# One transformer block: the seven-product stage of the second MLP matrix, reordered, with turned signs and two of its four sums formed by adding transfers

## The chip, the cores and the metric

The kernel runs on one core of one Trainium2 chip. The time is the device time of one execution in microseconds. The kernel before took 2019.21 us, the median of 3 runs (2017.92 to 2019.24).

## What is computed

One trunk layer on 512 tokens of width 2048, all in float32:

```
h = layer_norm(x, ln_in_g, ln_in_b)
u = h @ w_in                                   # pool values | q | k | v
m = concat(multi_scale_pool(u_pool), stick_breaking_attention(q, k, v)) @ w_out
h = layer_norm(2**0.25 * h + m, ln1_g, ln1_b)
f = square(relu(h @ w_ff1 + b_ff1))            # 512 x 8192
f = f @ w_ff2 + b_ff2                          # the stage that is changed
h = layer_norm(2**0.25 * h + f, ln2_g, ln2_b)
```

Only the product `f @ w_ff2` (8192 x 2048, "W_2" below) and the sums that go into it are changed.

## The kernel before

A float32 product is made of three matmuls of rounded parts: each operand is split into a high part (a copy to the type fp32r, on ScalarE) and a low part (the rest, a subtraction on VectorE), and `three` (L280 to L284) issues high x high, high x low and low x high into one bank of PSUM.

W_2's stage saves products in the manner of Strassen and Winograd: f and W_2 are cut into 2 x 2 blocks, and 7 block products take the place of 8. The inner dimension of 8192 is cut into 16 blocks of 512, four blocks make a slice (`slice_of`, L764), and there are four slices s = 0 to 3. A block is a unit u = 0 to 3 of its slice. W_2's 2048 columns are four groups q of 512: groups 0 and 1 are the left half, 2 and 3 the right half. One pass n = 0 or 1 takes the column pair (n, n + 2). For each (n, u) there are four pieces of W_2, 512 KB each: b11 and b12 (upper half of the inner block, left and right column), b21 and b22 (lower half).

The products, with A for blocks of f: P1 = A11 b11; P5 = S1 (b12 - b11); P6 = S2 (b22 - b12 + b11); P3 = S4 b22; P7 = S3 (the sum of P6, less b11); P2 = A12 b21; P4 = A22 (b21 less the sum of P6). S1 to S4 are sums of blocks of f. One product of one (n, u) is 12 matmuls, so a slice has 7 x 2 x 4 x 12 = 672, and the stage 2688.

How the pieces travel:

- `operands` (L678) runs after each block of the stage before. It squares the ReLU, forms S1 to S4 on VectorE (L690), splits all seven and writes them to DRAM (`f_d`, GpSimd's queue, L698).
- `operand` (L721) loads them again, 512 KB per unit and operand, through GpSimd's queue into a ring of 16 buffers named `o` (L716); four of these are free during the stage before.
- `w2_unit` (L731) loads a piece of W_2 through SyncE's queue into a ring of 10 buffers (tag `raw`, 3 + 7). b11 is loaded twice, once for P1 and once for P7 (tile `b11b`).
- `parts` (L739) splits a piece: `th` on ScalarE (L743), `tl` on VectorE (L744). The split tiles have 2 + 2 buffers each.
- The running sum of a unit sits in a tile `c` of its own (tag `c{n}{u}`). VectorE changes it or reads it four times per (n, u), 128 x 1024 elements each: L788 in `five`, L797 in `six_three`, L807 in `seven`, L825 in `four`.
- The banks of PSUM are two pairs `x` and two pairs `v` or `w`, all eight. `accumulate` (L756) adds a finished product to the output tiles `acc`.

The order of the work is set by the code's order and by a scheduler that places what stands under `high_priority` (L767) earlier than written; each engine and each queue then runs its own list in order. A slice runs P1 and P5 for n = 0, then n = 1; P6 and P3; P7; P2 and P4, each with n as the outer loop. The last slice runs P2, the first two normed output blocks (`norm_out`, L902), P7 and P4 at its end, and P4 is done by halves of the tokens.

Of the kernel before, what the change touches and what calls it, by code (L numbers as in the profile page):

```python
# [9 lines left out]
F32 = mybir.dt.float32  # L10
F32R = mybir.dt.float32r
AF = mybir.ActivationFunctionType
ALU = mybir.AluOpType
# [10 lines left out]
def block_kernel(  # L24
# [60 lines left out]
    def f(ap):  # L85
        return ap.bitcast(F32)
# [578 lines left out]


    mixing.close()
    first = pool(ctx, "first", 4, side="right")
# [9 lines left out]
    def operands(b, banks):  # L678
# [41 lines left out]

    def operand(s, *os):  # L721

        ops = [[] for _ in os]
        for u in range(PER):
            for n, o in enumerate(os):
                t = place(f"o{s}_{o}_{u}")
                nc.gpsimd.dma_start(f(t), f_d[s][u][o].rearrange("h p t -> p h t"))  # L727
                ops[n].append(t.rearrange("p h (i t) -> p h i t", i=2))
        return ops

    def w2_unit(b, half, q, name):  # L731

        k0 = b * N + half * H2
        early_one = turn("raw", 3, 10)
        raw = (wp if early_one else right).tile([P, 2, N], F32, tag="raw", bufs=3 if early_one else 7, name=name)
        nc.sync.dma_start(raw, w2[k0:k0 + H2, q * N:(q + 1) * N].rearrange("(c p) n -> p c n", p=P))
        return raw

    def parts(t, name, ring=False):  # L739
# [24 lines left out]
    def slice_of(s):  # L764
# [4 lines left out]
        x = [pair(f"x{s}_{n}", f"x{n}") for n in range(2)]  # L769
        v = [pair(f"v{s}_{n}", f"v{n}") for n in range(2)]  # L770
        chain = {}
# [11 lines left out]
        def five(n, u, b11):  # L783
            b, at, e = step(n, u)
            with ahead():
                b12 = w2_unit(b, 0, n + 2, f"b12_{at}")
                c = chain[n, u] = right.tile([P, 2, N], F32, tag=f"c{n}{u}", bufs=1, name=f"c_{at}")
                nc.vector.tensor_tensor(c, b12, b11, op=ALU.subtract)  # L788
                p5 = parts(c, f"5_{at}")
# [21 lines left out]
        def two(n, u):  # L811
            b, at, e = step(n, u)
            with ahead():
                b21 = w2_unit(b, 1, n, f"b21_{at}")
                p2 = parts(b21, f"2_{at}")
            times(w[n], A12, u, p2, *e)
            return b21

        def four(n, u, b21=None, ring=False):
            b, at, _ = step(n, u)  # L820
            with ahead():
                if b21 is None:
                    b21 = w2_unit(b, 1, n, f"b21b_{at}")
                c = chain[n, u]
                nc.vector.tensor_tensor(c, b21, c, op=ALU.subtract)  # L825
                return parts(c, f"4_{at}", ring)

        with ahead():
            A11, S1 = operand(s, 0, 3)
        for n in range(2):  # L830
            if s == 0 and n == 0:
                for us in (0, 1), (2, 3):
                    for u, b11 in [(u, one(n, u)) for u in us]:
                        five(n, u, b11)
            else:
                for u in units:
                    five(n, u, one(n, u))
            accumulate(x[n], 0, n)
            accumulate(v[n], 2, n + 2)
        with ahead():  # L840
            S2, S4 = operand(s, 4, 6)
        for n in range(2):
            for u in units:
                six_three(n, u)
            accumulate(x[n], 0, n + 2)
            accumulate(v[n], 0, n + 2)
        w = [pair(f"w{s}_{n}", f"v{n}") for n in range(2)]
        if not end:
            with ahead():
                S3, = operand(s, 5)  # L850
            for n in range(2):
                for u in units:
                    seven(n, u)
                accumulate(x[n], 2, n + 2)
            with ahead():
                A12, A22 = operand(s, 1, 2)
            for n in range(2):
                for u in units:
                    b21 = two(n, u)
                    times(x[n], A22, u, four(n, u, b21), False, u == PER - 1)  # L860
                accumulate(w[n], 0, n)
                accumulate(x[n], 2, n)
            return
        with ahead():
            A12, = operand(s, 1)
        for n in range(2):
            for u in units:
                two(n, u)
            accumulate(w[n], 0, n)
# [5 lines left out]
        for n in range(2):  # L875
            for u in units:
                seven(n, u)
            accumulate(x[n], 2, n + 2)
        with ahead():
            A22, = operand(s, 2)  # L880
        p4 = {}
        for t in range(2):
            for n in range(2):
                for u in units:
                    if t == 0:
                        p4[n, u] = four(n, u, ring=n == 1)
# [61 lines left out]
```

## Time and profile before

| | us |
|---|---|
| median of 3 runs | 2019.21 |
| the profiled execution, whole | 2015.19 |
| its span, first to last instruction | 2013.5 |
| W_2's stage, from the first of its matmuls | 1329.3 |
| its last matmul ends | 1997.0 |
| matmuls of the stage | 2688 |

The span is what the rows are measured in. The profiled execution is 4 us below the median of the runs, so a difference found in the rows is taken from 2019.21 and not from the span. TensorE is busy for nearly the whole span, and its matmuls overlap, so what counts in it is how many matmuls a stretch holds and where it sat idle. In slice 0 of the stage the share of the 16 DMA engines' time that packets took is near or above 1.00 (packets of two queues overlap on an engine).

### The profile page before, as it was taken

The numbers are of one execution on the slowest core, as the hardware profiler recorded it, in microseconds if no ns is written. First come the engines' busy times: TensorE is split into PE (matmuls) and PEld (weight loads), VectorE is DVE, ScalarE is ACT, GpSimd is POOL, SyncE is SP. The second block draws the span as 40 slices with busy tenths as digits, with TensorE's granted clock in tenths as the row PEclk, the third lists the DMA queues.
The fourth block names the chain that finished last, engine by engine and source line by source line (L and its number), as shares of the span: only waits on it lengthen the run. The fifth ranks groups of instructions, "written<-read, shape, count | busy, mean of one in ns | idle before, by whom it ended". The sixth has DMA issues, their size and how long they took to land.

```text
span 2013.5 us, 22312 instructions
## 1 busy us (share of the span) xinstructions
PE 1937.6 (96%) x8736; PEld 1592.4 (79%) x8736; DVE 1214.1 (60%) x1513; ACT 737.7 (37%) x898; POOL 169.3 (8%) x222
## 2 busy tenths in 40 slices
PE   6999999999999999999999999978999999999995
PEld 4888888877889988888888888856888778778874
DVE  8445565675459644544444444446977677678689
ACT  3344555552124233333333333323333333333331
POOL 5000000000000110010000001021111101101100
PEclk8999999999999999999999999989999999999998
DMA  5122222235344455556555556659676567577562
GB/s 221 32 86 82 84 84 84 74 99 188 105 141 135 159 188 169 174 182 207 191 175 168 167 170 210 201 202 370 216 263 226 176 233 242 178 238 242 194 224 84
DMA packets 157225, 345.47 MB, mean 172 GB/s; under 512 B 10688, under 2 KB 28224, under 8 KB 156736
## 3 DMA queue, kind: packets, MB, share of 16 engines
q1 hardware_dynamic: 124912, 224.43, 34.5%
q0 software_dynamic: 32064, 119.55, 16.4%
q8 instruction: 69, 1.13, 0.2%
q14 instruction: 36, 0.29, 0.0%
q10 hardware_dynamic: 144, 0.07, 0.0%
HBM read 281.09 MB, written 62.91 MB: 171 GB/s over the span
## 4 chain that ended last, share of the span: by engine, by line
PE 46%; issue 25%; DVE 14%; DMA 12%; POOL 2%; SPq 1%; ACT 0%; DVEq 0%; POOLq 0%; ACTq 0%
PE qk L361 9%; DMA b<-in_w_ff_dram 8%; PE f L210 7%; PE o L210 6%; DVE tl L744 5%; PE p L210 4%; DMA b11b<-in_w_ff_dram 4%; PE x L283 4%; PE o L283 3%; PE v L283 3%; PE f L283 2%; PE v L210 2%; POOL f_d L698 2%; DVE b11b L807 1%; DVE acc L759 1%
## 5 line engine op out<-in xcount | busy, mean ns | idle before, releaser
L210 PE MATMUL f<-h1l,wh_f 128*128 128x512 f32 x960 | 373.5, 389 | 0.0
L210 PE MATMUL f<-h1h,wh_f 128*128 128x512 f32 x960 | 373.5, 389 | 0.0
L210 PE MATMUL f<-h1h,wl_f 128*128 128x512 f32 x960 | 349.1, 389 | 0.0
L184 DVE TENSOR_TENSOR wl_f<-raw_f,wh_f 128x1024 fp32r<-128x1024 f32 x120 | 146.8, 1224 | 325.0 <-ACT wh_f L183 325.0
L283 PE MATMUL x<-th,o 128*128 128x512 f32 x1024 | 332.9, 394 | 9.1 <-DMA o<-f_d 7.2
L183 ACT CAST wh_f<-raw_f 128x1024 fp32r<-128x1024 f32 x120 | 126.4, 1053 | 392.1 <-PE f L210 374.2
L283 PEld LDWEIGHTS x<-th,o 128*128 128x128 f32 x1024 | 193.3, 189 | 52.5 <-issue 7.6
L283 PE MATMUL x<-tl,o 128*128 128x512 f32 x512 | 203.3, 397 | 11.9 <-DVE tl L744 11.9
L210 PEld LDWEIGHTS f<-h1h,wh_f 128*128 128x128 f32 x960 | 180.3, 188 | 37.5
L210 PEld LDWEIGHTS f<-h1h,wl_f 128*128 128x128 f32 x960 | 180.1, 188 | 37.4
L210 PEld LDWEIGHTS f<-h1l,wh_f 128*128 128x128 f32 x960 | 180.2, 188 | 37.3
L283 PE MATMUL v<-th,o 128*128 128x512 f32 x512 | 169.7, 395 | 7.4 <-ACT th L743 7.4
L743 ACT CAST th<-b 128x1024 fp32r<-128x1024 f32 x96 | 101.1, 1053 | 188.8 <-PE v L283 59.2
L743 ACT CAST th<-c 128x1024 fp32r<-128x1024 f32 x96 | 100.8, 1052 | 161.9 <-PE x L283 109.8
L744 DVE TENSOR_TENSOR tl<-b,th 128x1024 fp32r<-128x1024 f32 x96 | 116.9, 1219 | 25.4 <-ACT th L743 25.4
L698 POOL DMA_DIRECT2D f_d<-fh x32 | 30.4, 951 | 1209.6 <-ACT fh L695 1209.6
L283 PEld LDWEIGHTS x<-tl,o 128*128 128x128 f32 x512 | 96.9, 189 | 39.7 <-DVE tl L744 18.8
L744 DVE TENSOR_TENSOR tl<-c,th 128x1024 fp32r<-128x1024 f32 x96 | 116.8, 1219 | 14.0 <-ACT th L743 13.8
L727 POOL DMA_DIRECT2D o<-f_d x112 | 81.2, 725 | 491.6 <-PE x L283 299.8
L283 PEld LDWEIGHTS v<-th,o 128*128 128x128 f32 x512 | 97.1, 190 | 29.0 <-ACT th L743 8.2
L283 PE MATMUL v<-tl,o 128*128 128x512 f32 x256 | 101.8, 398 | 7.8 <-DVE tl L744 7.7
L361 PE MATMUL qk<-hTl,wh_qk 128*128 128x512 f32 x256 | 99.9, 390 | 0.0
(208 smaller groups left out, 3243.4 us busy)
## 6 DMA issues: line engine op xcount, KB each, us to landing
b<-in_w_ff_dram SPq DMA_DIRECT2D x128, 512.0 KB, 4.8
raw_f<-in_w_ff_dram SPq DMA_DIRECT2D x120, 512.0 KB, 3.9
o<-f_d POOLq DMA_DIRECT2D x112, 512.0 KB, 5.6
f_d<-fh POOLq DMA_DIRECT2D x32, 896.0 KB, 5.7
f_d<-fl POOLq DMA_DIRECT2D x32, 896.0 KB, 9.4
raw_qk<-in_w_in_dram SPq DMA_DIRECT2D x64, 256.0 KB, 2.9
b11b<-in_w_ff_dram SPq DMA_DIRECT2D x32, 512.0 KB, 4.2
raw_o<-in_w_out_dram SPq DMA_DIRECT2D x24, 512.0 KB, 3.7
```

The costliest lines, as they stand in the source:

```text
L183: nc.scalar.copy(h, raw)
L184: nc.vector.tensor_tensor(l, raw, f(h), op=ALU.subtract)
L210: mm = nc.tensor.matmul(bank, a, b, start=first and n == 0, stop=last and n == 2)
L283: mm = nc.tensor.matmul(bank, l, r, start=first and n == 0, stop=last and n == 2, skip_group_check=free)
L361: nc.tensor.matmul(bank, a, b, start=kc == 0 and n == 0, stop=kc == KC - 1 and n == 2)
L698: nc.gpsimd.dma_start(f_d[b // PER][b % PER][:, n, :, i * H2:(i + 1) * H2].rearrange("o p t -> p o t"), f(t))
L727: nc.gpsimd.dma_start(f(t), f_d[s][u][o].rearrange("h p t -> p h t"))
L743: nc.scalar.copy(h, t)
L744: nc.vector.tensor_tensor(l, t, f(h), op=ALU.subtract)
L759: nc.vector.tensor_tensor(a, a, banks[t], op=ALU.add)
L807: nc.vector.tensor_tensor(b11, chain[n, u], b11, op=ALU.subtract)
```

## The change

The pieces' sums are now all positive: S1, S2 and S4 are formed with the other sign, and the right half of the output is subtracted instead of added. So P5 takes b11 + b12, P6 that plus b22, P7 b22 + b12, and P4 the sum of P6 plus b21. A sum of two pieces can then be made by a transfer that adds to what lies in its destination, and two of the four are: b12 is added to b11's tile for P5 (but for the first three pieces of slice 0), and b12 is added to b22's tile for P7. These adding transfers are issued on GpSimd's queue. In the last slice P4's sum is formed so too. b11 is loaded straight into its `c` tile, and its second load is gone.

In each product the column pairs n = 0, 1 now are the inner loop and the units the outer one. In slices 0 to 2 P4 of a unit comes ahead of its P2. The last slice begins with P2. In slice 0 the loads of S2 and S4 wait for the second P1.

```diff
-        for o, x, y, op in ((s1, a21, a22, ALU.add), (s2, s1, a11, ALU.subtract),
-                            (s3, a11, a21, ALU.subtract), (s4, a12, s2, ALU.subtract)):
-            nc.vector.tensor_tensor(o, x, y, op=op)
+        nc.vector.tensor_tensor(s1, a22, a21, op=ALU.subtract)
+        nc.vector.scalar_tensor_tensor(s2, s1, -1.0, a11, op0=ALU.mult, op1=ALU.subtract)
+        nc.vector.tensor_tensor(s3, a11, a21, op=ALU.subtract)
+        nc.vector.scalar_tensor_tensor(s4, s2, -1.0, a12, op0=ALU.mult, op1=ALU.subtract)
...
+    def add_unit(t, b, half, q):
+        nc.gpsimd.dma_start(t, w2_at(b, half, q), accum_op=ALU.add)
...
-            nc.vector.tensor_tensor(a, a, banks[t], op=ALU.add)
+            nc.vector.tensor_tensor(a, a, banks[t], op=ALU.add if q < 2 else ALU.subtract)
...
         def one(n, u):
             b, at, e = step(n, u)
             with ahead():
-                b11 = w2_unit(b, 0, n, f"b11_{at}")
-                p1 = parts(b11, f"1_{at}")
-            times(x[n], A11, u, p1, *e)
-            return b11
+                if s == 0 and 2 * u + n < 3:
+                    b11[n, u] = w2_unit(b, 0, n, f"b11_{at}")
+                    p1 = parts(b11[n, u], f"1_{at}")
+                else:
+                    c = chain[n, u] = right.tile([P, 2, N], F32, tag=f"c{n}{u}", bufs=1, name=f"c_{at}")
+                    nc.sync.dma_start(c, w2_at(b, 0, n))
+                    p1 = parts(c, f"1_{at}")
+                    add_unit(c, b, 0, n + 2)
+            begun.append(times(x[n], A11, u, p1, *e))
...
-        def six_three(n, u):
+        def six(n, u):
...
-                b22 = w2_unit(b, 1, n + 2, f"b22_{at}")
+                b22[n, u] = w2_unit(b, 1, n + 2, f"b22_{at}")
                 c = chain[n, u]
-                nc.vector.tensor_tensor(c, b22, c, op=ALU.subtract)
+                nc.vector.tensor_tensor(c, c, b22[n, u], op=ALU.add)
                 p6 = parts(c, f"6_{at}")
-                p3 = parts(b22, f"3_{at}")
+                if end:
+                    add_unit(c, b, 1, n)
             times(x[n], S2, u, p6, False, u == PER - 1)
+
+        def three_(n, u):
+            with ahead():
+                p3 = parts(b22[n, u], f"3_{s}_{n}_{u}")
+                add_unit(b22[n, u], s * PER + u, 0, n + 2)
             times(v[n], S4, u, p3, False, u == PER - 1)
 
         def seven(n, u):
...
-                b11 = w2_unit(b, 0, n, f"b11b_{at}")
-                nc.vector.tensor_tensor(b11, chain[n, u], b11, op=ALU.subtract)
-                p7 = parts(b11, f"7_{at}")
+                p7 = parts(b22[n, u], f"7_{at}")
...
+        if end:
+            w = [pair(f"w{s}_{n}", f"v{n}") for n in range(2)]
+            with ahead():
+                A12, = operand(s, 1)
+            both(two, units)
+            every(w, 0, 0)
...
-        for n in range(2):
-            if s == 0 and n == 0:
-                for us in (0, 1), (2, 3):
-                    for u, b11 in [(u, one(n, u)) for u in us]:
-                        five(n, u, b11)
-            else:
-                for u in units:
-                    five(n, u, one(n, u))
+        for us in (0, 1), (2, 3):
+            both(one, us)
+            both(five, us)
...
-            S2, S4 = operand(s, 4, 6)
-        for n in range(2):
-            for u in units:
-                six_three(n, u)
+            S2, S4 = operand(s, 4, 6, behind=None if s else begun[1])
+        for u in units:
+            both(six, (u,))
+            both(three_, (u,))
...
-            for n in range(2):
-                for u in units:
-                    seven(n, u)
-                accumulate(x[n], 2, n + 2)
+            both(seven, units)
+            every(x, 2, 2)
             with ahead():
-                A12, A22 = operand(s, 1, 2)
-            for n in range(2):
-                for u in units:
-                    b21 = two(n, u)
-                    times(x[n], A22, u, four(n, u, b21), False, u == PER - 1)
+                A22, A12 = operand(s, 2, 1)
+            for u in units:
+                both(two, (u,), both(four, (u,)))
```

Two places where the lists of the engines change. Names are tile, slice, and for W_2's tiles pass n and unit u; `o0_4_1` is operand 4 (S2) of unit 1 in slice 0.

VectorE, slice 1, around P7. Before:

```order
L744 TENSOR_TENSOR tl_6_1_1_0_11280<-c_1_1_0_10980,th_6_1_1_0_11279 128x1024
L807 TENSOR_TENSOR b11b_1_1_1_11529<-c_1_1_1_11018,b11b_1_1_1_11529 128x1024
L744 TENSOR_TENSOR tl_3_1_1_0_11284<-b22_1_1_0_11276,th_3_1_1_0_11283 128x1024
L759 TENSOR_TENSOR acc0_3674<-acc0_3674,x1_0_0_10780 128x512
L759 TENSOR_TENSOR acc1_3675<-acc1_3675,x1_0_1_10781 128x512
L744 TENSOR_TENSOR tl_6_1_1_1_11315<-c_1_1_1_11018,th_6_1_1_1_11314 128x1024
L759 TENSOR_TENSOR acc0_3674<-acc0_3674,v1_0_0_10784 128x512
L759 TENSOR_TENSOR acc1_3675<-acc1_3675,v1_0_1_10785 128x512
L807 TENSOR_TENSOR b11b_1_1_2_11548<-c_1_1_2_11056,b11b_1_1_2_11548 128x1024
```

And after the change, VectorE, slice 1, P7:

```order
L756 TENSOR_TENSOR tl_7_1_0_0_11386<-b22_1_0_0_11077,th_7_1_0_0_11385 128x1024
L771 TENSOR_TENSOR acc0_3674<-acc0_3674,x1_1_0_10751 128x512
L771 TENSOR_TENSOR acc1_3675<-acc1_3675,x1_1_1_10752 128x512
L756 TENSOR_TENSOR tl_7_1_1_0_11402<-b22_1_1_0_11096,th_7_1_1_0_11401 128x1024
L771 TENSOR_TENSOR acc0_3674<-acc0_3674,v1_0_0_10753 128x512
L848 TENSOR_TENSOR c_1_0_1_10811<-c_1_0_1_10811,b21_1_0_1_11603 128x1024
L771 TENSOR_TENSOR acc1_3675<-acc1_3675,v1_0_1_10754 128x512
L756 TENSOR_TENSOR tl_7_1_0_1_11418<-b22_1_0_1_11149,th_7_1_0_1_11417 128x1024
```

Before, the subtraction of `b11b` for P7 stood among the splits of P6 and P3, eight places ahead of its own split; now P7's splits read `b22` as it is, and the additions of `b21` for P4 stand among them.

GpSimd's queue at the start of slice 0. Before:

```order
L727 DMA o0_6_2_10014<-f_d0_2_5519 128x2x512
L727 DMA o0_4_3_10016<-f_d0_3_5520 128x2x512
L727 DMA o0_6_3_10018<-f_d0_3_5520 128x2x512
L727 DMA o0_5_0_10312<-f_d0_0_5517 128x2x512
L727 DMA o0_5_1_10314<-f_d0_1_5518 128x2x512
L727 DMA o0_5_2_10316<-f_d0_2_5519 128x2x512
```

And after:

```order
L731 DMA o0_6_2_9999<-f_d0_2_5519 128x2x512
L731 DMA o0_4_3_10001<-f_d0_3_5520 128x2x512
L731 DMA o0_6_3_10003<-f_d0_3_5520 128x2x512
L749 DMA c_0_1_1_9746<-in_w_ff2_dram 128x2x512
L731 DMA o0_5_1_10307<-f_d0_1_5518 128x2x512
L749 DMA c_0_0_2_9841<-in_w_ff2_dram 128x2x512
L731 DMA o0_5_2_10309<-f_d0_2_5519 128x2x512
L749 DMA c_0_1_2_9860<-in_w_ff2_dram 128x2x512
L731 DMA o0_2_0_10445<-f_d0_0_5517 128x2x512
L749 DMA c_0_0_3_9879<-in_w_ff2_dram 128x2x512
L731 DMA o0_5_3_10311<-f_d0_3_5520 128x2x512
L749 DMA c_0_1_3_9898<-in_w_ff2_dram 128x2x512
```

The five adding transfers that P5 of slice 0 needs (L749) stand behind all twelve operand loads of P1, P5, P6 and P3; before, P5's second pieces came through SyncE's queue.

## Rows read from the trace of the kernel before

**Rows 1.** The profile's page, busy time by engine.
```profile
PE 1937.6 (96%) x8736; PEld 1592.4 (79%) x8736; DVE 1214.1 (60%) x1513; ACT 737.7 (37%) x898; POOL 169.3 (8%) x222
```

**Rows 2.** Stretches: length, busy us (count) by engine, granted clock, DMA share, GB/s.
```profile
core 0: us, PE busy (x) PEld busy (x) DVE busy (x) ACT busy (x) POOL busy (x), PEclk, DMA share, GB/s
1329.30:1511.30 182.00, 161.74 (x672) 129.31 (x673) 134.71 (x130) 63.98 (x61) 32.03 (x43) 0.94 0.79 283
1511.30:1673.60 162.30, 156.36 (x673) 125.31 (x673) 118.89 (x116) 58.98 (x56) 20.27 (x28) 1.00 0.66 222
1673.60:1836.00 162.40, 157.05 (x673) 125.16 (x672) 118.81 (x116) 58.96 (x56) 20.28 (x28) 1.00 0.66 219
1836.00:1997.00 161.00, 155.11 (x673) 125.44 (x672) 130.11 (x154) 56.09 (x56) 11.60 (x17) 1.00 0.53 176
1450.00:1500.00 50.00, 50.00 (x219) 40.69 (x218) 37.45 (x38) 18.97 (x18) 5.07 (x7) 1.00 0.73 247
1340.00:1350.00 10.00, 4.85 (x12) 3.09 (x12) 3.62 (x4) 1.43 (x2) 6.03 (x8) 0.67 1.00 339
1340.00:1400.00 60.00, 46.35 (x171) 35.36 (x171) 32.65 (x33) 16.33 (x17) 15.12 (x21) 0.84 1.03 396
```

**Rows 3.** Waits of TensorE, 1329 to 1997 us: total us, times, longest.
```profile
PE x L283 <- DVE tl L744: 11.9, 12, 3.7
PE v L283 <- DVE tl L744: 7.7, 10, 2.0
PE v L283 <- ACT th L743: 7.4, 2, 7.2
PE x L283 <- DMA o<-f_d: 7.2, 1, 7.2
```

**Rows 4.** Chain of waits around 1570 us: start us, us, what.
```profile
1571.46 3.69 DMA b11b<-in_w_ff_dram
...
1575.24 1.23 DVE b11b L807
1576.47 1.14 DVE tl L744
...
1577.63 3.58 DMA b11b<-in_w_ff_dram
```

**Rows 5.** Page, groups: VectorE's four sums and the splits (count, busy us, mean ns, idle before).
```profile
L744 DVE TENSOR_TENSOR tl<-b,th 128x1024 fp32r<-128x1024 f32 x96 | 116.9, 1219 | 25.4 <-ACT th L743 25.4
L743 ACT CAST th<-b 128x1024 fp32r<-128x1024 f32 x96 | 101.1, 1053 | 188.8 <-PE v L283 59.2 <-PE x L283 48.1 <-PE w L283 47.2
L788 DVE TENSOR_TENSOR c<-b,b 128x1024 f32<-128x1024 f32 x32 | 39.2, 1224 | 50.2 <-DMA b<-in_w_ff_dram 48.5 <-issue 1.7
L807 DVE TENSOR_TENSOR b11b<-c,b11b 128x1024 f32<-128x1024 f32 x32 | 39.0, 1222 | 43.9 <-DMA b11b<-in_w_ff_dram 43.9
L797 DVE TENSOR_TENSOR c<-b,c 128x1024 f32<-128x1024 f32 x32 | 39.0, 1222 | 14.4 <-DMA b<-in_w_ff_dram 14.2
L825 DVE TENSOR_TENSOR c<-b,c 128x1024 f32<-128x1024 f32 x24 | 29.3, 1221 | 16.6 <-DMA b<-in_w_ff_dram 16.4
```

**Rows 6.** Transfers, 1340 to 1380 us: packets and MB by queue; issue to landing.
```profile
q0 software_dynamic: 2625, 9.64, 63.8%
q1 hardware_dynamic: 3092, 5.97, 38.7%
...
o<-f_d POOLq DMA_DIRECT2D x13, 512.0 KB, 16.6
```

**Rows 7.** GpSimd in time, 1340 to 1363 us: operand loads of slice 0.
```profile
1341.37 4.36 POOL L727 DMA_DIRECT2D o<-f_d  x6
...
1352.74 0.72 POOL L727 DMA_DIRECT2D o<-f_d  x1 [4.29 <-DMA f_d<-fl]
...
1361.97 0.72 POOL L727 DMA_DIRECT2D o<-f_d  x1 [2.73 <-DMA o<-f_d]
```

**Rows 8.** Transfers, 1450 to 1550 us: count, KB each, median us to landing.
```profile
o<-f_d POOLq DMA_DIRECT2D x17, 512.0 KB, 5.1
```

**Rows 9.** Chain of waits from 1985 us.
```profile
1987.36 5.39 DVE acc L910 x8
1992.75 1.79 DVE acc L759 x3
```

More of the change, by code (lines that the diff above doesn't have):

```diff
@@ L719, in place, with operand @@
         return (first if at_first else right).tile([P, 2, N], dt, tag="o", bufs=4 if at_first else 12, name=name)
-    def operand(s, *os):
+    def operand(s, *os, behind=None):
         ops = [[] for _ in os]
@@ L726, in operand, with w2_at @@
                 t = place(f"o{s}_{o}_{u}")
-                nc.gpsimd.dma_start(f(t), f_d[s][u][o].rearrange("h p t -> p h t"))
+                load = nc.gpsimd.dma_start(f(t), f_d[s][u][o].rearrange("h p t -> p h t"))
+                if behind:
+                    after(load, behind)
                 ops[n].append(t.rearrange("p h (i t) -> p h i t", i=2))
         return ops
+    def w2_at(b, half, q):
+        k0 = b * N + half * H2
+        return w2[k0:k0 + H2, q * N:(q + 1) * N].rearrange("(c p) n -> p c n", p=P)
     def w2_unit(b, half, q, name):
-        k0 = b * N + half * H2
         early_one = turn("raw", 3, 10)
         raw = (wp if early_one else right).tile([P, 2, N], F32, tag="raw", bufs=3 if early_one else 7, name=name)
-        nc.sync.dma_start(raw, w2[k0:k0 + H2, q * N:(q + 1) * N].rearrange("(c p) n -> p c n", p=P))
+        nc.sync.dma_start(raw, w2_at(b, half, q))
         return raw
+    def add_unit(t, b, half, q):
+        nc.gpsimd.dma_start(t, w2_at(b, half, q), accum_op=ALU.add)
     def parts(t, name, ring=False):
@@ L769, in slice_of @@
         x = [pair(f"x{s}_{n}", f"x{n}") for n in range(2)]
-        v = [pair(f"v{s}_{n}", f"v{n}") for n in range(2)]
-        chain = {}
+        begun = []
+        chain, b22, b11 = {}, {}, {}
         def step(n, u):
@@ L815, in two, with fourth @@
                 p2 = parts(b21, f"2_{at}")
             times(w[n], A12, u, p2, *e)
-            return b21
-        def four(n, u, b21=None, ring=False):
+        def fourth(n, u, ring=False):
             b, at, _ = step(n, u)
             with ahead():
[L822 to L826, printed above, removed]
+                b21, c = None, chain[n, u]
+                if not end:
+                    b21 = w2_unit(b, 1, n, f"b21_{at}")
+                    nc.vector.tensor_tensor(c, c, b21, op=ALU.add)
+                return b21, parts(c, f"4_{at}", ring)
@@ new lines, in four, with both, every @@
+        def four(n, u):
+            b21, p4 = fourth(n, u)
+            times(x[n], A22, u, p4, False, u == PER - 1)
+            return b21
+        def both(what, units, *more):
+            return {(n, u): what(n, u, *(m[n, u] for m in more)) for u in units for n in range(2)}
+        def every(banks, tb0, q0):
+            for n in range(2):
+                accumulate(banks[n], tb0, q0 + n)
+        if end:
[4 more added lines that the diff above has]
+            every(w, 0, 0)
@@ L828, in slice_of @@
+        v = [pair(f"v{s}_{n}", f"v{n}") for n in range(2)]
         with ahead():
             A11, S1 = operand(s, 0, 3)
-        for n in range(2):
-            if s == 0 and n == 0:
-                for us in (0, 1), (2, 3):
-                    for u, b11 in [(u, one(n, u)) for u in us]:
-                        five(n, u, b11)
-            else:
-                for u in units:
-                    five(n, u, one(n, u))
-            accumulate(x[n], 0, n)
-            accumulate(v[n], 2, n + 2)
@@ L840, in slice_of @@
-        with ahead():
-            S2, S4 = operand(s, 4, 6)
-        for n in range(2):
-            for u in units:
-                six_three(n, u)
-            accumulate(x[n], 0, n + 2)
-            accumulate(v[n], 0, n + 2)
-        w = [pair(f"w{s}_{n}", f"v{n}") for n in range(2)]
+        for us in (0, 1), (2, 3):
+            both(one, us)
+            both(five, us)
+        every(x, 0, 0)
+        every(v, 2, 2)
+        with ahead():
+            S2, S4 = operand(s, 4, 6, behind=None if s else begun[1])
@@ L848, in slice_of @@
+        for u in units:
+            both(six, (u,))
+            both(three_, (u,))
+        every(x, 0, 2)
+        every(v, 0, 2)
         if not end:
+            w = [pair(f"w{s}_{n}", f"v{n}") for n in range(2)]
             with ahead():
                 S3, = operand(s, 5)
-            for n in range(2):
-                for u in units:
-                    seven(n, u)
-                accumulate(x[n], 2, n + 2)
+            both(seven, units)
+            every(x, 2, 2)
             with ahead():
-                A12, A22 = operand(s, 1, 2)
@@ L870, in slice_of @@
+            for u in units:
+                both(two, (u,), both(four, (u,)))
+            every(x, 2, 0)
+            every(w, 0, 0)
+            return
         with ahead():
@@ L874, in slice_of @@
             norm_out(tb)
[L875 to L878, printed above, removed]
+        both(seven, units)
+        every(x, 2, 2)
         with ahead():
@@ L885, in slice_of @@
                     if t == 0:
-                        p4[n, u] = four(n, u, ring=n == 1)
+                        p4[n, u] = fourth(n, u, ring=n == 1)[1]
                     times(x[n], A22, u, p4[n, u], False, u == PER - 1, (t,))
```

24 lines of the change are left out of this document (9 added, 15 removed).

## The prediction

> **What bounds the kernel now.** I read the busy line first, then the stretches by slice, TensorE's waits, the chain of waits, and the transfers by queue. TensorE is busy 96% of the span, VectorE 60% [rows 1]; but a busy share says nothing of what a full pace would be. For that look at a stretch without a gap: 219 matmuls in 50.00 us, 0.2283 us each at clock 1.00 [rows 2]. A slice has 672, so 153.4 us at that pace. The four slices took 182.0, 162.3, 162.4 and 161.0 [rows 2]: 28.6, 8.9, 9.0 and 7.6 us above it, 54.1 in all. That is all a change of order and sums can win, beside the 16.5 us from the last matmul (1997.0) to the end of the span (2013.5).
>
> Two causes show. In slice 0 the excess is the start: from 1340 to 1350 only 12 matmuls ran, at clock 0.67, while the DMA share was 1.00 [rows 2], and the two longest waits, 7.2 us each, are for a split on ScalarE and an operand load [rows 3]. From 1340 to 1400 it is 171 matmuls, where full pace has 263 [rows 2]. Transfers bound that stretch. In the later slices the waits are many and short, for the low parts `tl` from VectorE: 22 of them in the two rows, 19.6 us [rows 3]. The chain shows why: the second load of b11 (3.69 us), its subtraction (1.23), a split (1.14) that frees the buffer for the next load (3.58) [rows 4]. One turn takes 1577.63 - 1571.46 = 6.2 us, and it must go round once per (n, u), for P6 and P3, whose 24 matmuls want 24 x 0.2283 = 5.5 us. VectorE does its list in order, so a subtraction that waits for its load holds up the splits behind it: the four sums waited 48.5, 43.9, 14.2 and 16.4 us for loads [rows 5].
>
> **The change part by part.**
>
> Sums on VectorE. Before, 128: three lines of 32, one of 24, and 8 more of the last slice. After: 3 for P5 (the first pieces), 32 for P6, 24 for P4, so 59. The 69 that go are 69 x 1.22 = 84 us of VectorE [rows 5]. Little of that is time by itself, since VectorE has 40% idle [rows 1]; what counts is the loop above, and it goes whole: no second b11, no subtraction ahead of the splits. The ring of ten now takes 16 pieces a slice where it took 40 (b11 goes into `c`, b12 is added), so its loads run a ring's length ahead.
>
> What is late next in slices 1 and 2? VectorE's list around P7 now has the addition of b21 among the splits, and its load can be issued two units ahead; with VectorE busy some 70% of the slice before (118.89 of 162.3 us [rows 2]) and 16 additions x 1.22 = 20 us fewer, I leave 1 us of excess in each (0 to 3). So 8.9 + 9.0 becomes 2: 16 us gained. In slice 3, 24 additions leave, 29 us of its 130.11 [rows 2]; of its 7.6 I leave 2: 5.6 gained. Running the column pairs inside moves bank changes: P7 to P4 writes on into `x` banks that VectorE has just read, and slice 3 starts with P2 on banks just freed. Each is two reads of a bank pair within 12 matmuls (2.7 us) of slack: 0 to 1 us, taken as part of the 1 and 2 left. The multiply-and-subtract forms in `operands` have as many instructions as before, beside matmuls of the stage before: nothing.
>
> Adding transfers in steady state. No row shows one. The nearest rows from both sides: a plain 512 KB load takes 5.1 us where the queues are at ease [rows 8], 16.6 where they are full [rows 6]. P5's can be issued once P1's split has read `c`, P7's once P3's split has read `b22`: the lists give both some 14 us before the matmuls need the result. I take 7 us, near the easy row, and it is hidden; at 16.6 it would not be. Room on the engines: slices 1 and 2 moved 222 GB/s x 162.3 us = 36.0 MB, and at the 396 GB/s of the full stretch [rows 2] 153.4 us carry 60.7 MB. The number of transfers is the same as before (five per (n, u)), 16 of them adding, 8.4 MB. If such a one holds the engines m times as long as a load, the slice needs 36.0 + 8.4 (m - 1): 44.4 at m = 2, 61 at m = 4. I take m = 2 and keep 1 and 4.
>
> The Trainium skill has a price for this: "Collectives: The Full Stack", in "The bandwidth ceiling: the fold count and why AG ≠ RS ≠ AR", says that an add within a transfer needs two source reads per chunk, and that this, not the add, halves the rate. By it m would be 2; no run here shows it yet.
>
> The start of slice 0. P5 of five pieces now waits for adding transfers on GpSimd's queue, behind twelve operand loads, as the order of that queue shows. The first six of those were issued from 1341.37, the next waited 4.29 us for a write of f's operands, the last was issued at 1361.97 [rows 7], and a load took 16.6 us to land [rows 6]. So the twelfth lands at about 1378.6, and the first sum behind it. GpSimd's queue moved 9.64 MB in 40 us, 241 GB/s [rows 6]: 2.2 us per 512 KB, 4.3 for an adding one at m = 2. 1378.6 + 4.3 = 1382.9, plus a split on ScalarE and VectorE (1.05 + 1.22 [rows 5]), 1385. The matmuls that need it are number 108 on (P1, P1, P1, P1, P5 of four, five in), at full pace 1329.3 + 108 x 0.2283 = 1354. Lag 31 us. The four sums after it come 4.3 to 6.5 us apart (an operand load lies between): the last at about 1404, ready 1406, wanted by matmul 204 at 1375.9: lag 30. So I put slice 0's excess at 31, against 28.6: 2.4 us lost. Bounds: 14 if GpSimd's queue gets more of the engines while SyncE's later loads, which now wait for `c` tiles and the writes of f's operands, are away; 45 if less. The wait of the loads for S2 and S4 behind the second P1 costs nothing: that P1 can end at 1329.3 + 24 x 0.2283 = 1334.8, before the first operand load that I count.
>
> The end. Before, the chain went through one normed block's 8 instructions on VectorE (5.39 us, to 1992.75) and an addition behind them (1.79), 4 us before the last matmul ended [rows 9]; with 8 additions fewer in that P4 VectorE comes to them sooner. I take 1.5 us of the 16.5 (0 to 3).
>
> Sum: the excess goes from 54.1 to 31 + 1 + 1 + 2 = 35, a gain of 19, and 1.5 at the end: 20.5 us. The profiled execution took 2015.2, which would be 1994.7; the median of the runs is 4.0 us above it, and from 2019.2 I get 1998.7.
>
> **The rivals.**
>
> A, slower: an adding transfer holds the engines four times as long as a load. The place is the start of slice 0, then slice 3, which has 24 of them. At m = 4 a sum takes 8.7 us there instead of 4.3 and its neighbour's load still 2.2: the last of five comes at 1378.6 + 8.7 + 4 x 10.9 = 1431, ready 1433, lag 57; with a part of that hidden, excess 54, 25 more than before. Slice 3 moved 176 x 161.0 = 28.3 MB; with 24 x 0.524 x 3 more, 66 MB, 167 us at 396 GB/s: 6 lost. Slices 1 and 2 still win 16, the end 1.5: 14 us slower, 2033. It decides from about m = 3.5. For it: the start is the one stretch where the engines are full already. Against it: nothing in the trace needs such a factor.
>
> B, faster by less: the queues share by packets. From 1340 to 1380 they had 2625 and 3092 packets, near equal turns, though 9.64 and 5.97 MB: packets of 3.7 and 1.9 KB [rows 6]. W_2's pieces come in the short rows, so the sums on GpSimd's queue would have half the engines, 198 GB/s: 5.3 us each at m = 2, 7.5 with a load between. The last is at 1378.6 + 5.3 + 30 = 1414, ready 1416, lag 40: 9 us more, 2008.
>
> The Trainium skill's "DMA: Bandwidth & Descriptors", in "Queues, rings and completion order", says the same: an engine goes round between the queues with work, a packet from each. The trace agrees with it there (2625 against 3092); whether SyncE's queue has work all that time is what decides.
>
> C, no change: the loop only changes its name. An adding transfer of 16.6 us is not hidden by 14, and the split of its sum, at the head of VectorE's and ScalarE's lists, holds up those behind it as the second b11 did. 2.6 us once per unit pair and slice, and in each of three slices about 8 us: the gain of slices 1 to 3 (21.6) is eaten, 2020. Against it: steady queues show 5.1 [rows 8].
>
> D, faster by more: the start gains as well. If SyncE's fewer early loads leave the engines to GpSimd's queue, its twelve loads, 6.3 MB, take 16 us at 396 GB/s and land by 1362 (the last write of f's operands lets them go at 1352.7 [rows 7]), 17 us sooner; slice 0's excess is 14 and the time 1982.
>
> **How the numbers follow.** Forecast 50%: its own range 1988 to 2008, from the bounds of the small terms and most of the start's. A 18%, B 12%, C 12%, D 8%. Low 1984 leaves out half of D (4%) and a little of the forecast; high 2028 cuts off the outer part of A (12%). A measurement can tell about 0.2%, 4 us, from no change. Faster by more: the forecast, B and D, 70%. Within: nearly all of C, 11%. Slower: A and the rest of C, 19%.
>
> **What would show it.** Right: slices 1 and 2 of about 154 to 156 us, hardly a wait for `tl`, no chain from load to sum to split; adding transfers of 7 us or so in slice 1; slice 0 of about 184 us, with TensorE waiting around 1355 to 1385 on splits whose releasers are adding transfers; 69 fewer sums on VectorE. Wrong: adding transfers over 14 us in slices 1 to 3 (C), GpSimd's queue or the DMA share near 1.00 in slice 3 (A), or a slice 0 under 175 or over 195 us, which would say that the queue's share was misjudged. That start is the term I trust least.

## The result and the profile after

The changed kernel took 2002.74 us (median of 4 runs, 2000.24 to 2003.92), before 2019.22 in the same series (4 runs). The ratio is 0.9917, with a 95% interval of 0.9901 to 0.9933: 16.5 us faster. The forecast was 1998.7, in a range of 1984 to 2028. The profiled execution is one of 2003.92 us with a span of 2002.2; that of before had a span of 2013.5 and was 4 us quicker than its runs' median, and that of after 1.2 us slower than its own, so the two traces differ by 11.3 us where the runs differ by 16.5. What follows adds up the 11.3.

The page, busy time by engine, beside [rows 1]:

```profile
PE 1938.8 (97%) x8736; PEld 1598.5 (80%) x8736; DVE 1143.6 (57%) x1444; ACT 737.0 (37%) x898; POOL 253.8 (13%) x291
```

VectorE has 69 instructions and 70.5 us fewer, GpSimd 69 issues more. Then the slices, and the full stretch at the start, beside [rows 2] (same columns):

```profile
1329.10:1521.00 191.90, 165.19 (x673) 131.16 (x674) 114.85 (x112) 63.80 (x61) 50.55 (x59) 0.92 0.87 277
1521.00:1676.20 155.20, 154.82 (x674) 125.80 (x673) 102.74 (x101) 58.90 (x56) 39.98 (x45) 1.00 0.82 230
1676.20:1835.20 159.00, 156.09 (x674) 127.00 (x673) 102.86 (x101) 58.73 (x56) 37.44 (x42) 0.99 0.81 230
1835.20:1989.00 153.80, 153.60 (x673) 125.76 (x671) 115.14 (x146) 56.12 (x56) 40.78 (x41) 1.00 0.71 169
...
1340.00:1400.00 60.00, 40.37 (x135) 30.77 (x136) 25.01 (x23) 12.05 (x12) 19.13 (x23) 0.74 1.05 357
```

Slice 0 became 9.9 us longer; slices 1 to 3 became 7.1, 3.4 and 7.2 us shorter. The tail went from 16.5 to 13.4 us. From 1340 to 1400 only 135 matmuls ran, not 171. In slices 1 and 2 the DMA share is 0.82 and 0.81 at almost the old rate in GB/s, where it was 0.66.

TensorE's waits in the stage, beside [rows 3]:

```profile
PE v L283 <- ACT th L755: 15.3, 2, 9.1
PE x L283 <- DVE tl L756: 5.7, 6, 2.0
PE x L283 <- ACT th L755: 3.5, 1, 3.5
PE v L283 <- DVE tl L756: 3.1, 1, 3.1
```

22 waits for `tl` have become 7, 8.8 us in all. What is left is two long waits at the start, behind a split on ScalarE. There GpSimd's queue is the place to look; here it is in time (start, us, what; in brackets the idle time before and what ended it):

```profile
1362.46 1.24 POOL L749 DMA_DIRECT2D c<-in_w_ff_dram  x1 [1.48 <-issue]
...
1366.28 1.20 POOL L749 DMA_DIRECT2D c<-in_w_ff_dram  x1 [1.17 <-issue]
...
1370.14 1.21 POOL L749 DMA_DIRECT2D c<-in_w_ff_dram  x1 [1.19 <-issue]
1372.08 0.74 POOL L731 DMA_DIRECT2D o<-f_d  x1 [0.73 <-DMA o<-f_d]
1387.42 1.22 POOL L749 DMA_DIRECT2D c<-in_w_ff_dram  x1 [14.61 <-DVE tl L756]
```

Three adding transfers go out behind the operand loads, with one more load between each two. The fourth waits 14.61 us: it may not write its tile until P1's split has read it. On ScalarE that split stands behind the split of the first sum, which landed at 1379.6. On VectorE it stands behind two sums for P6 (L816) that wait for their loads of b22:

```profile
1379.62 1.23 DVE L816 TENSOR_TENSOR c<-c,b 128x1024 f32<-128x1024 f32 x1 [2.75 <-DMA b<-in_w_ff_dram]
1383.62 1.23 DVE L816 TENSOR_TENSOR c<-c,b 128x1024 f32<-128x1024 f32 x1 [2.77 <-DMA b<-in_w_ff_dram]
1384.76 2.35 DVE L756 TENSOR_TENSOR tl<-c,th 128x1024 fp32r<-128x1024 f32 x2
```

The first of the two splits in the last line is P5's low part, the one that TensorE waits 3.1 us for; the second is P1's, which lets the fourth transfer go at 1387.42. TensorE resumes at 1386.03 and then has no wait until 1409.6, so the trace shows no cost of the 14.61 us themselves.

And in slice 2, VectorE, one stall (the same columns), and TensorE right behind it:

```profile
1781.55 1.23 DVE L848 TENSOR_TENSOR c<-c,b 128x1024 f32<-128x1024 f32 x1 [2.42 <-DMA b<-in_w_ff_dram]
1782.69 1.22 DVE L756 TENSOR_TENSOR tl<-b,th 128x1024 fp32r<-128x1024 f32 x1
```

```profile
1783.96 0.79 PE L283 MATMUL x<-tl,o 128*128 128x512 f32 x1 [2.04 <-DVE tl L756]
1784.55 1.05 PE L283 MATMUL x<-th,o 128*128 128x512 f32 x2
1785.40 0.63 PE L283 MATMUL x<-tl,o 128*128 128x512 f32 x1
```

The sum with b21 stands ahead of P7's split and waits for its load; TensorE loses 2.04 us, and then runs its next eight matmuls at the lower of its two clock levels (1783.96 to 1787.20 has a granted clock of 0.50). A wait of 2 us cost about 3.8, read from how far TensorE lay behind full pace before and after it.

Issue to landing, whole program (median us, last column):

```profile
o<-f_d POOLq DMA_DIRECT2D x112, 512.0 KB, 7.2
b<-in_w_ff_dram SPq DMA_DIRECT2D x70, 512.0 KB, 5.5
...
c<-in_w_ff_dram POOLq DMA_DIRECT2D x37, 512.0 KB, 8.9
...
b<-in_w_ff_dram POOLq DMA_DIRECT2D x32, 512.0 KB, 8.7
```

Adding transfers (the two POOLq lines on `in_w_ff`) take 8.7 to 8.9 us.

### The profile page after: what moved, and what is told of

Same layout as the page of the kernel before. It is cut to its first block, busy times and chain, and to the rows that moved or that the text cites. A ratio compares the mean times of both kernels' runs of the same rounds, so it can differ in the third digit from the quotient of the medians.

```text
span 2002.2 us, 22330 instructions
## 1 busy us (share of the span) xinstructions
PE 1938.8 (97%) x8736; PEld 1598.5 (80%) x8736; DVE 1143.6 (57%) x1444; ACT 737.0 (37%) x898; POOL 253.8 (13%) x291
## 3 DMA queue, kind: packets, MB, share of 16 engines
q0 software_dynamic: 50832, 155.73, 26.6%
## 4 chain that ended last, share of the span: by engine, by line
PE 86%; issue 5%; DVE 4%; DMA 3%; POOL 1%; ACT 0%; SPq 0%; DVEq 0%; POOLq 0%
PE f L210 33%; PE x L283 12%; PE qk L361 9%; PE o L210 6%; PE v L283 5%; PE p L210 4%; PE w L283 4%; PE o L283 3%; PE f L283 2%; PE v L210 2%; DMA o<-f_d 2%; DMA b<-in_w_ff_dram 1%; DVE tl L756 1%; PE z L283 1%; PE v L276 1%
## 5 line engine op out<-in xcount | busy, mean ns | idle before, releaser
L755 ACT CAST th<-c 128x1024 fp32r<-128x1024 f32 x125 | 130.9, 1052 | 231.1 <-PE x L283 113.5
L283 PE MATMUL x<-tl,o 128*128 128x512 f32 x512 | 203.4, 398 | 5.9 <-DVE tl L756 5.7
L756 DVE TENSOR_TENSOR tl<-c,th 128x1024 fp32r<-128x1024 f32 x125 | 152.1, 1222 | 98.0 <-ACT th L755 97.4
L731 POOL DMA_DIRECT2D o<-f_d x112 | 93.3, 838 | 334.4 <-PE x L283 208.7
```

The lines of the kernel that those rows point to most:

```text
L283: mm = nc.tensor.matmul(bank, l, r, start=first and n == 0, stop=last and n == 2, skip_group_check=free)
L731: load = nc.gpsimd.dma_start(f(t), f_d[s][u][o].rearrange("h p t -> p h t"))
L755: nc.scalar.copy(h, t)
L756: nc.vector.tensor_tensor(l, t, f(h), op=ALU.subtract)
```

## The experiments

The theory was the prediction's: the adding transfers take the second b11 and its sum away, and with them the loop of load, sum, split. The rival: another part of the change, the order or the ring, did it. Times are medians of 4 to 8 runs, ratios are to the kernel before on the same chip. Slices are read as in [rows 2].

**1. Slice 0's P5 on VectorE alone** (`s0_vector`).

```diff
-                if s == 0 and 2 * u + n < 3:
+                if s == 0:
```

> The changed kernel, but all eight sums of P5 in slice 0 (not only the first three) are added on VectorE from a load of b12 on SyncE's queue; the other 27 sums by transfers of slices 1 to 3 and all of P7's stay. In the profile of the changed kernel slice 0 took 191.9 us, 38.4 above full pace, against 28.6 before. Theory (the five adding transfers behind the operand loads cost the start 10 us): slice 0 falls to 180 to 184 us, slices 1 to 3 stay as in the changed kernel, time about 1993 us, ratio to before 0.987. Rival (the start is bound by the bytes that must come, wherever they are added): slice 0 stays at 188 to 192 us, time 2000 to 2004, ratio 0.991.

Measured 1995.17 us, ratio 0.9880 (0.9859 to 0.9900); slices 187.2, 156.5, 155.6, 153.8. Faster, but of slice 0's loss only 4.7 us came back, so neither expectation holds for the slice. Here b11 and b12 both go through the ring of ten; experiment 7, with b11 in `c`, has a slice 0 that is 6.0 us shorter still.

**2. Plain loads in the adding transfers' place** (`plain_loads`).

```diff
-        nc.gpsimd.dma_start(t, w2_at(b, half, q), accum_op=ALU.add)
+        nc.gpsimd.dma_start(t, w2_at(b, half, q))
```

> Each adding transfer is a plain load of the same piece into the same tile on the same queue, so the sum is replaced by its last piece; order, waits and bytes written are the same. Theory (an adding transfer holds the engines about 1.9 times as long as a load, and only the start feels it): DMA share of slices 1, 2 and 3 falls from 0.82, 0.81, 0.71 to about 0.66, 0.66, 0.5; slice 0 gets 4 to 8 us shorter, slices 1 to 3 within 3 us of 155.0, 159.0, 154.0; time about 1997, ratio 0.989. Rival (adding costs nothing, its place in the queue all): share and slice 0 stay, time 2001 to 2004, ratio 0.991 to 0.992. Second rival (slower landing of adding transfers makes the waits in slices 1 and 2): slices 1 and 2 fall to 154 together with slice 0.

Measured 1992.48 us, ratio 0.9864 (0.9841 to 0.9887). The slices:

```profile
1329.50:1516.00 186.50, 161.77 (x673) 130.45 (x674) 114.86 (x112) 64.20 (x61) 42.91 (x58) 0.92 0.80 288
1516.00:1669.60 153.60, 153.60 (x674) 126.03 (x673) 102.74 (x101) 58.90 (x56) 31.84 (x44) 1.00 0.69 233
1669.60:1823.20 153.60, 153.60 (x673) 126.07 (x672) 102.96 (x101) 58.89 (x56) 30.38 (x42) 1.00 0.69 234
1823.20:1977.00 153.80, 153.77 (x673) 125.88 (x671) 115.32 (x145) 56.12 (x56) 28.97 (x41) 1.00 0.50 170
```

and the landings, same columns as above:

```profile
o<-f_d POOLq DMA_DIRECT2D x112, 512.0 KB, 5.5
...
c<-in_w_ff_dram POOLq DMA_DIRECT2D x37, 512.0 KB, 5.3
```

The difference to the changed kernel is the price of adding by itself: 5.4 us in slice 0, 1.6 in slice 1, 5.4 in slice 2, nothing in slice 3. Each kernel has one trace, and the figures of slices 1 and 2 are not firm: `s0_vector` has the same adding transfers there, and its slices are 2.9 and 2.0 us above those with plain loads. In slice 0 the price does not fall on the first sum: at matmul 120 TensorE lags 33.0 us behind full pace with plain loads and 33.1 in the changed kernel. The second rival (slices 1 and 2 too) was nearest. Slice 1 gives the size: 0.82 x 155.2 - 0.69 x 153.6 = 21.3 us of all engines for 16 transfers, 1.33 us each beyond a load; a load of 0.524 MB takes 1.32 at the 396 GB/s of [rows 2]. So an adding transfer holds the engines twice as long as a load. The rule of the Trainium skill ("Collectives: The Full Stack", "The bandwidth ceiling: the fold count and why AG ≠ RS ≠ AR") that an add reads two sources and so halves the rate agrees with it.

**3. The order without adding transfers** (`order_only`).

```diff
                     p1 = parts(c, f"1_{at}")
-                    add_unit(c, b, 0, n + 2)
...
+                    b12 = w2_unit(b, 0, n + 2, f"b12_{at}")
+                    nc.vector.tensor_tensor(chain[n, u], chain[n, u], b12, op=ALU.add)
...
-                add_unit(b22[n, u], s * PER + u, 0, n + 2)
...
-                p7 = parts(b22[n, u], f"7_{at}")
+                b11b = w2_unit(b, 0, n, f"b11b_{at}")
+                nc.vector.tensor_tensor(b11b, chain[n, u], b11b, op=ALU.subtract)
+                p7 = parts(b11b, f"7_{at}")
```

> The changed kernel's order and signs, but no adding transfers: b12 is loaded on SyncE and added on VectorE, b11 is loaded a second time and subtracted for P7 as before, b21 is added on VectorE in the last slice too (128 sums on VectorE again). Theory (the second b11 and its sum at the head of VectorE's list made the loop of 6.2 us): slices 1 and 2 go back to 160 to 163 us, slice 0 to 180 to 184, time 2010 to 2017, ratio 0.996 to 0.999. Rival (the order of units and pairs removed the waits, not the adding transfers): slices 1 and 2 stay at 154 to 157, slice 0 at 180 to 184, time about 1993, ratio 0.987.

Measured 1997.56 us, ratio 0.9893 (0.9872 to 0.9914). The slices:

```profile
1330.30:1509.80 179.50, 161.94 (x673) 130.13 (x674) 129.05 (x126) 63.92 (x61) 32.05 (x43) 0.95 0.84 299
1509.80:1664.70 154.90, 153.84 (x674) 126.00 (x673) 119.18 (x118) 58.93 (x56) 20.27 (x28) 1.00 0.68 231
1664.70:1820.20 155.50, 154.03 (x674) 125.94 (x673) 118.84 (x117) 58.88 (x56) 20.27 (x28) 1.00 0.70 231
1820.20:1982.30 162.10, 156.38 (x673) 127.19 (x671) 139.57 (x165) 55.95 (x56) 11.60 (x17) 0.98 0.48 162
```

The theory falls: VectorE has its 128 sums again, b11 is loaded twice, and slices 1 and 2 are as short as in the changed kernel. Only slice 3 is not: at its end VectorE does sums, splits and the normed blocks without a gap, 139.57 us busy, and 8.7 us go there.

**4. Adding transfers, pairs outer again** (`pairs_apart`).

```diff
-        for us in (0, 1), (2, 3):
-            both(one, us)
-            both(five, us)
+        for n in range(2):
+            for us in (0, 1), (2, 3):
+                for u in us:
+                    one(n, u)
+                for u in us:
+                    five(n, u)
...
```

P6 and P3 follow the same pattern, and in slices 0 to 2 also P7, and P2 with P4. Slice 0's three pieces on VectorE are now the first three of n = 0.

> The changed kernel with the adding transfers, but the column pairs are the outer loop again in slices 0 to 2 and in P1, P5, P6 and P3 of slice 3 (P7 and the last slice's P2 and P4 as changed). Theory (the adding transfers do it): slices 1 and 2 at 154 to 158 us, slice 0 at 188 to 195, time 2000 to 2006, ratio 0.991 to 0.993. Rival (the order does it): slices 1 and 2 back at 160 to 163, time 2012 to 2018, ratio 0.997 to 0.999.

Measured 2038.37 us, ratio 1.0093 (1.0073 to 1.0113), slower than before; slices 203.4, 163.1, 163.3, 163.9. ScalarE in slice 1 (total, times, longest):

```profile
ACT th L755 <- DMA c<-in_w_ff_dram: 35.9, 7, 8.4
```

With one pair at a time a unit's P5 starts two products after its P1, 5.5 us, where an adding transfer needs 8.9. ScalarE's splits queue up behind its landing. With both pairs inside it starts four products after, 11 us, and the transfer fits.

Slice 0's longest wait is of another kind. TensorE waits for P5's low part, and VectorE, ahead of that split, stands on a sum with b21 for P4 whose load has not landed:

```profile
PE v L283 <- DVE tl L756: 14.1, 1, 14.1
1408.64 1.23 DVE L848 TENSOR_TENSOR c<-c,b 128x1024 f32<-128x1024 f32 x1 [12.69 <-DMA b<-in_w_ff_dram]
```

**5 and 6. Order or ring?** In `order_only` b11 also goes straight into `c`, so its ring takes 32 tiles a slice, not 40. Two kernels part the two. `order_ring` is `order_only` with b11 in the ring:

```diff
-                    c = chain[n, u] = right.tile([P, 2, N], F32, tag=f"c{n}{u}", bufs=1, name=f"c_{at}")
-                    nc.sync.dma_start(c, w2_at(b, 0, n))
-                    p1 = parts(c, f"1_{at}")
+                    b11[n, u] = w2_unit(b, 0, n, f"b11_{at}")
+                    p1 = parts(b11[n, u], f"1_{at}")
```

> The kernel with the new order and without adding transfers (1997.6 us, slices 179.5, 154.9, 155.5, 162.1), but b11 is loaded into the ring of ten again and P5's sum goes to the c tile, so the ring takes 40 tiles a slice as in the kernel before, not 32. Theory 1 (the order alone took the loop away): slices 1 and 2 stay at 154 to 157 us, time 1996 to 2000, ratio 0.989. Theory 2 (the eight tiles fewer in the ring did it, loads run ahead): slices 1 and 2 go back to 159 to 163, time 2005 to 2014, ratio 0.994 to 0.997.

`before_c` is the kernel before with b11 in `c`, and nothing else:

```diff
-                b11 = w2_unit(b, 0, n, f"b11_{at}")
+                b11 = chain[n, u] = right.tile([P, 2, N], F32, tag=f"c{n}{u}", bufs=1, name=f"c_{at}")
+                nc.sync.dma_start(b11, ...)
...
-                c = chain[n, u] = right.tile([P, 2, N], F32, tag=f"c{n}{u}", bufs=1, name=f"c_{at}")
-                nc.vector.tensor_tensor(c, b12, b11, op=ALU.subtract)
+                c = b11
+                nc.vector.tensor_tensor(c, b12, c, op=ALU.subtract)
```

> The kernel before in its own order, with one thing changed: b11 is loaded straight into the c tile and P5's sum is formed in place, so the ring of ten takes 32 tiles a slice, not 40. Theory 1 (order): slices 1 and 2 stay at 160 to 163 us, time 2014 to 2020, ratio 0.998 to 1.001. Theory 2 (ring): slices 1 and 2 fall to 154 to 157, time 2002 to 2008, ratio 0.991 to 0.994. Both can hold in part: then each of the two kernels gives about half.

`order_ring`: 2013.19 us, ratio 0.9966 (0.9952 to 0.9979), slices 185.6, 153.6, 156.8, 175.2. `before_c`: 2000.39 us, ratio 0.9901 (0.9886 to 0.9916), slices 169.2 (its stage begins 8.2 us later, so that is 177.4), 157.3, 156.2, 161.5. In slices 1 and 2 either one alone takes most of the loss away, so both theories hold there, and not by halves: of 17.9 us above full pace `order_ring` keeps 3.6 and `before_c` 6.7. In slice 0 the ring alone helps (177.4 against 182.0) and in slice 3 it changes nothing; the new order with 40 tiles is slower than before in both. One edit to the kernel before is worth as much as the whole change. VectorE's waits for loads in slice 1, the kernel before:

```profile
DVE b11b L807 <- DMA b11b<-in_w_ff_dram: 17.9, 8, 4.3
DVE c L788 <- DMA b<-in_w_ff_dram: 13.3, 7, 3.6
DVE c L825 <- DMA b<-in_w_ff_dram: 6.3, 3, 5.0
DVE c L797 <- DMA b<-in_w_ff_dram: 3.8, 3, 2.3
```

and `before_c`:

```profile
DVE b11b L809 <- DMA b11b<-in_w_ff_dram: 9.3, 6, 3.2
DVE c L827 <- DMA b<-in_w_ff_dram: 8.3, 4, 3.8
```

41.3 us become 17.6: the sums of P5 and P6 wait for no load any more. `order_ring` has 23.2 us of such waits left. How the loop fares is seen in the chain of waits around 1570 us, beside [rows 4]. In `before_c` it is still there:

```profile
1565.28 3.76 DMA b11b<-in_w_ff_dram
...
1573.74 1.23 DVE tl L744
1574.98 3.58 DMA b11b<-in_w_ff_dram
```

and in `order_ring` it has gone from the chain, which is TensorE alone:

```profile
1569.85 5.44 PE x L283 x24
```

In both, the second b11's loads now go out in pairs. Before, they were issued one at a time, every 6 to 8 us in slice 1 (1563.6, 1571.5, 1577.6); in `before_c` two close together every 10 us (1565.3 and 1566.5, 1575.0 and 1578.4), in `order_ring` likewise (1570.2 and 1572.2, 1580.4 and 1583.1). The products P6 and P3 of two pieces want 11.0 us, so a turn with a pair in it is short enough. Which part of the new order does it, units outside or another, was not tried apart.

**7. P5's sums on VectorE everywhere, P7's by transfers** (`p5_vector`).

```diff
-                    add_unit(c, b, 0, n + 2)
...
+                else:
+                    b12 = w2_unit(b, 0, n + 2, f"b12_{at}")
+                    nc.vector.tensor_tensor(chain[n, u], chain[n, u], b12, op=ALU.add)
```

> The changed kernel, but P5's sums are added on VectorE in all slices, in place in the c tile, from a load of b12 on SyncE's queue; P7's 32 sums and the last slice's eight for P4 stay adding transfers (40, not 69). Theory (in slice 0 P5's adding transfers cost the 7 to 12 us, by their place behind the operand loads and by their length; P7's are hidden): slice 0 at 179 to 182 us, slices 1 to 3 at 154 to 157, time 1988 to 1991, ratio 0.985. Rival (P7's adding transfers cost as well, by filling the engines in slices 0 and 2): slice 0 at 184 to 188 or slices 1 and 2 at 156 to 160, time 1993 to 1998, ratio 0.988.

Measured 1989.01 us, ratio 0.9845 (0.9828 to 0.9861); slices 181.2, 155.2, 156.1, 153.8. As the theory had it. It differs from experiment 1 in slice 0 mainly by b11 in `c`, which is 6 us there. So slice 0's 10.7 us above this kernel in the changed one are, by the totals, half the adding (5.4, experiment 2, which takes it from P7's transfers as well) and half the place in GpSimd's queue.

**8. Only the last eight sums by transfers** (`last_add`): `order_only`, with

```diff
+                if end:
+                    add_unit(chain[n, u], b, 1, n)
```

behind the sum for P7, and no b21 for P4 in the last slice.

> The kernel with the new order and without adding transfers, but the eight sums of the last slice's P4 are formed by adding transfers, as in the changed kernel; 8 adding transfers in all, not 69. Theory (only those eight pay: they take 8 sums from VectorE where the normed output blocks keep it busy, 8 us): slice 3 falls from 162.1 to 154 us, the rest stays, time 1989, ratio 0.985. Rival (slice 3 of the changed kernel gained by the other 16 adding transfers, too, or these eight land too late behind them): slice 3 at 158 to 162, time 1994 to 1998, ratio 0.988.

Measured 1998.27 us, ratio 0.9888 (0.9871 to 0.9906); slices 180.2, 154.4, 153.7, 165.9. A miss: P4 lost 1.2 us where it lost 8.7, but P6 and P3 lost 11 ahead of it: their splits stand behind VectorE's sums for P7, which wait for the second b11 (1900 to 1960 us):

```profile
DVE b11b L831 <- DMA b11b<-in_w_ff_dram: 15.9, 4, 7.2
```

In `order_only` P6 and P3 lost nothing there. The loads were issued at about the same times, but beside the adding transfers they took twice as long to land (1885 to 1930 us, median; `order_only` first):

```profile
b11b<-in_w_ff_dram SPq DMA_DIRECT2D x6, 512.0 KB, 4.8
b11b<-in_w_ff_dram SPq DMA_DIRECT2D x6, 512.0 KB, 9.2
```

**9. P7 and P4 by transfers in the last slice only** (`end_only`): `p5_vector`, with

```diff
-                add_unit(b22[n, u], s * PER + u, 0, n + 2)
+                if end:
+                    add_unit(b22[n, u], s * PER + u, 0, n + 2)
```

and the second b11 for P7 in slices 0 to 2.

> The kernel with P5's sums on VectorE (1989.0 us, slices 181.2, 155.2, 156.1, 153.8), but P7's sums of slices 0 to 2 by the second load of b11 and VectorE, as in the kernel before; adding transfers only for P7 and P4 of the last slice, 16 in all, not 40. Theory (P7's adding transfers are hidden and save nothing in slices 0 to 2): slices 0 to 2 within 2 us of 181.2, 155.2, 156.1, slice 3 at 154, time 1987 to 1991, ratio 0.984 to 0.986. Rival (the second b11 costs waits even in the new order): slices 1 and 2 at 158 or more, time over 1994.

Measured 1987.78 us, ratio 0.9836 (0.9820 to 0.9853): the lowest of all, 0.8% below the changed kernel, but not clear of `p5_vector`, whose interval overlaps. Slices 179.7, 156.8, 153.7, 153.8. In slices 0 to 2 P7's 24 adding transfers are worth nothing; in slice 3 the 16 for P7 and P4 give 8.3 us against `order_only`.

**10. P7's adding transfer twice** (`twice`): `p5_vector`, with

```diff
+                for _ in range(2):
-                add_unit(b22[n, u], s * PER + u, 0, n + 2)
+                    add_unit(b22[n, u], s * PER + u, 0, n + 2)
```

> The kernel with P5's sums on VectorE (1989.0 us), but each adding transfer for P7 is issued twice, the second waiting for the first, so P7's operand holds b12 twice and the product is another. 32 more adding transfers of 512 KB. From the DMA shares (0.82 against 0.69 in slice 1 with 16 adding transfers or 16 plain loads in their place) one holds the engines 2.6 us, so the share of slices 1 and 2 rises by 8 x 2.6 / 155 = 0.13, from 0.75 to 0.88. Theory (P7's have over 20 us of room behind P3, and the engines too): slices 1 to 3 within 2 us, time 1989 to 1993. Rival (the room is used up, or the fuller engines delay SyncE's loads as in slice 2 of the changed kernel): slices 1 and 2 at 158 to 162, time 1996 to 2006.

Measured 2041.24 us, ratio 1.0103 (1.0082 to 1.0123); slices 195.3, 164.9, 165.4, 171.2. The theory failed. The share rose to 0.85, about as expected for the longer slice. The fuller engines show little: in slice 1 SyncE's loads into the ring landed in 5.8 us at the median, in `p5_vector` in 5.2. The long waits are others: each second transfer waits at the head of GpSimd's queue for the first to land, and what stands behind it waits too. GpSimd and ScalarE in slice 1:

```profile
POOL b L749 <- DMA b<-in_w_ff_dram: 24.7, 7, 6.7
```

```profile
ACT th L755 <- DMA b<-in_w_ff_dram: 24.1, 5, 12.5
```

## Why the prediction was right, and where it was not

The time and the sign were right, and the mechanism that it gave for the gain was not the one needed.

"It goes whole: no second b11, no subtraction ahead of the splits" is the step that failed as a cause. The loop did go, and slice 1 measured 1.8 us above full pace against the 1 forecast; but `order_only` keeps both, and its slices 1 and 2 are 1.5 and 2.1 us above full pace where they were 8.9 and 9.0. The prediction saw the chain load, sum, split, load [rows 4] and took out the sum; in its place the runs show that b11 in `c` or the new order is enough, and that with either the loads of the second b11 go out two at a time. That the pairs are the reason is read from the traces; no run changed them alone. The same paragraph named the ring's 16 tiles instead of 40, and did not ask whether that alone would do.

"The start of slice 0": 31 us of excess forecast, 38.5 measured. The sums came nearly as forecast: the first landed at 1379.6 (1382.9 forecast), the next 5.8, 5.9, 6.8 and 6.9 us apart (4.3 to 6.5), the last at 1405.0 (about 1404). TensorE lagged 27.0 us at matmul 108, against 31, but 33.9 at matmul 132. In between it waited 3.1 us for P5's low part, behind the sums for P6 and their late b22, and ran at the lower clock level (granted 0.50 from 1386.0 to 1391.3). So a sum that waits for its load ahead of a split, which was to go "whole", stood there again with b22 in the place of b11, and the forecast has no term for it. Later the lag grew to 36.3 at matmul 216, after a wait of 1.8 us for banks that VectorE had to read, and to 38.4 at the slice's end; there the forecast had the last sums, and TensorE waited for none of them. Rival B's 40 was nearer by accident: its equal shares do not show, as GpSimd's queue had 2977 packets from 1340 to 1380 and SyncE's 2303.

"I take m = 2": right, 2.0 by experiment 2. "I take 7 us, and it is hidden": it was 8.7 to 8.9, hidden in slices 1 and 3, not in slice 2, where 5.6 us of excess stand against 1 forecast and the experiment with plain loads has 0.2. The forecast priced full engines by the whole slice (44.4 of 60.7 MB); a single late load of b21 made some 3.8 of it. That is no fixed price: `s0_vector`, with the same transfers there, has an excess of 2.2.

Slice 3 had 0.4 us of excess, not 2, and the tail gave 3.1, not 1.5. VectorE's load at the end was the reason given. For slice 3 experiments 3 and 9 bear it out; for the tail they do not, since `order_only` keeps the sums and its tail is 14.2 us, so most of the gain there came with the order. In the traces the sum was 11.3 us, not 20.5: 11.3 less gained in the slices (46.3 of excess against 35), 1.6 more in the tail; the rest is rounding and a stage that began 0.2 us earlier. The runs show 16.5, because the profiled execution of before was one of its quick ones and that of after its slowest. So a good part of how near 1998.7 came is luck.

Rival A (a factor of four) and D (the start gains) are excluded by the same numbers. Rival C's mechanism, a split held up by the landing of an adding transfer, is real: it shows in `pairs_apart` and `twice`, both slower than before. The change escapes it by starting P5 four products after P1.

## What to carry to other kernels

When a chain of waits goes round through a ring of buffers, first try to give the ring fewer tiles to carry (one piece loaded straight to where its sum will stand was worth 19 us here, `before_c`); do that before the arithmetic is moved elsewhere. A sum within a transfer costs the DMA engines a second load's time and 3.5 us of landing; it pays where VectorE has no gap (the last slice), and not at a start that transfers bind, nor where less than about 9 us lie between the read of the old value and the use of the new one. Look also for sums that wait for a load ahead of a split in an engine's list: that stall was in the kernel before, and it came back in the changed kernel with b22 and b21 and in `last_add` with the second b11. When one edit brings several effects, price each by itself: the gain of slices 1 and 2 came with the order and with b11 in `c`, and only in the last slice with the adding transfers.

## What was not expected of the hardware

An adding transfer of 512 KB shows 128 more packets than a load of it: GpSimd's queue had 50832 packets with them and 42000 with plain loads, 8832 more for 69 transfers, at the same 155.73 MB. Issuing one keeps GpSimd 1.2 us, not 0.74. And plain loads on the same queue slow down beside them, from 5.5 to 7.2 us at the median, though the rate over slices 1 and 2 hardly differs.
